# An output projection by seven block products in place of eight

## The chip, the cores and the metric

The kernel runs on one core of one Trainium2 chip. The metric is the device time of one execution in microseconds. A core has five engines with their own instruction queues: PE (matrix products, with its weight loads shown as PEld), DVE (elementwise work), ACT (elementwise functions and copies), POOL (here it issues accumulating DMAs) and SP (it issues DMAs). They meet through semaphores.

## The reference

One layer of a decoder trunk over 512 tokens of width 1024. Five branches mix the tokens; each is projected up to width 1024, gated and summed into `merged`, and one output projection with a residual and a final RMSNorm ends the layer:

```python
gates = jax.nn.sigmoid(gate_logits).reshape(b, s, N_BRANCH, D_MODEL)
merged = jnp.zeros_like(x)
for n, y in enumerate((y_a, y_b, y_c, y_d, y_m)):
    merged = merged + gates[:, :, n] * (y @ w_up[n])
return x + merged @ w_out
...
return rmsnorm(x, final_norm_g)
```

`merged @ w_out` is a product of 512x1024 by 1024x1024. All arrays are float32.

## The kernel before

**Precision.** Each float32 operand f is kept as a pair: hi, f rounded by a copy on ACT, and lo = f - hi, by a subtraction on DVE. A product is three passes on PE, hi by hi, hi by lo and lo by hi (`mm3`, lines 199 to 201). So every block that PE is to read costs one ACT and one DVE instruction first, the split (`split_sb`, lines 217 and 218, for blocks in SBUF).

**Order of the work.** The branches are cut into steps, and the string STEPS lists them. G3 is the next 128 channels of the gate of branch 3 (24 matmuls), U3 the next 128 channels of its up-projection (12 matmuls, then on DVE the product with the gate, line 974, and the addition into `merged`, line 976). dn1 is the last step of branch 3's own scan. After dn1 come one U2, five G3 and eight U3; the last U3 completes channel block 7 of `merged`. Within this order a planner fixes each engine's queue before the run: it goes by the place of an instruction in the text, moved ahead by an offset for some (`PREP` for the splits of weights, `EVAC` for readings of PSUM), and by its own estimate of times. On the chip each queue runs strictly in that order.

**Weights.** A weight block is 128 partitions by 1024, 512 KB. SP loads it into the staging tile `wst`, of which there are two (WST), in the order of the steps; ACT and DVE split its halves into `whi` and `wlo`, of which there are six each (three blocks). For gates (`load_w_add`, lines 171 to 186) ACT copies hi and minus f, and a DMA of POOL's queue with an addition (line 183) makes lo. A slot of `wst` is free when its last copy is done, and a pair of `whi`, `wlo` when PE has used it.

**Output projection** (lines 1036 to 1115). `merged` holds channels on the partitions: 8 blocks of 128 channels by 512 tokens. All eight are split into mH, mL (lines 1062, 217, 218). W_out comes in two column halves of four loads each (`load_out`, line 1043; splits in lines 1050 and 1051 into woH, woL, eleven tiles each). For a column half and each of the four tiles of 128 tokens, eight channel blocks times three passes are summed in one PSUM bank of 128x512; the last token tile of the second half is done in two parts of 256 columns. Then DVE adds the bank to x (line 1085; x lies in the space of `merged`), ACT sums the squares (line 1088), DVE multiplies by the final gain (line 1103), and after the second half the root, its reciprocal and the scaling follow (lines 1092 to 1115), with half of a row scaled on DVE and half on ACT, and two output DMAs.

Of the kernel before, what the change touches and what calls it, by code (L numbers as in the profile page):

```python
# [16 lines left out]
P = 128  # L17
# [47 lines left out]
NWO = 11  # L65
# [16 lines left out]
def build(ctx, tc, x, mem, memT, cols_d, rows_d, wcm, wbv, wcv0, wcv1, wmk, wmv, wup, wout, dw, fg, out):  # L82
# [46 lines left out]
    hpool = ctx.enter_context(tc.tile_pool(name="hpool", bufs=1, side="right"))  # L129
# [17 lines left out]
    def f32(t):  # L147
        return t.bitcast(F32)
# [46 lines left out]
    def mm3(ps, terms, first=True, last=True, check=False):  # L195

        n = len(terms)
        for i, (ah, al, bh, bl) in enumerate(terms):
            mm(ps, lhsT=ah, rhs=bh, start=first and i == 0, stop=False, skip_group_check=check)  # L199
            mm(ps, lhsT=ah, rhs=bl, start=False, stop=False, skip_group_check=check)  # L200
            mm(ps, lhsT=al, rhs=bh, start=False, stop=last and i == n - 1, skip_group_check=check)  # L201
# [13 lines left out]
    def split_sb(f, hi, lo):  # L215

        act(hi, f, AF.Copy)
        V.tensor_tensor(out=lo, in0=f, in1=f32(hi), op=ALU.subtract)
# [730 lines left out]
    upw = {}  # L949

# [12 lines left out]
    def up(n, ys):  # L963
# [6 lines left out]
        mm3(ps, [(*piece(upw[n], 4 * (d % 2) + k, P, 4), *ys[k]) for k in range(NE)])  # L970
# [11 lines left out]
    def step(s):  # L982
# [41 lines left out]
        elif c == "U":  # L1024
            assert None not in ys[i]
            up(i, ys[i])
        else:
# [7 lines left out]

    epool = ctx.enter_context(tc.tile_pool(name="epool", bufs=1))
    mH = epool.tile([P, NK, S], F32R, name="mH")
    mL = epool.tile([P, NK, S], F32R, name="mL")
    nc.sync.dma_start(out=rows[:, :D], in_=fg.broadcast_to([P, D]))

    def load_out(half, k2):
        st = wpool.tile([P, 1056], F32, tag="wst", name="wst", bufs=WST)
        nc.sync.dma_start(out=st[:, :D], in_=wout[half, k2])
        res = []
        for kk in range(2):
            hi = epool.tile([P, S], F32R, tag="woH", name="woH", bufs=NWO)
            lo = epool.tile([P, S], F32R, tag="woL", name="woL", bufs=NWO)
            f = st[:, kk * S:(kk + 1) * S]
            with tc.high_priority(offset=PREP):
                act(hi, f, AF.Copy)  # L1050
                V.tensor_tensor(out=lo, in0=f, in1=f32(hi), op=ALU.subtract)
            res.append((hi, lo))
        return res

    last = ENDS.split()
    wo = []
    for d in range(NK):
        while min(ups.values()) <= d:
            step(last.pop(0))
        if d % 2 == 0:  # L1060
            wo += load_out(0, d // 2)
        split_sb(merged[:, d, :], mH[:, d, :], mL[:, d, :])
    xr, sums, quarter = [], {}, {}

    def parts_of(t):

        return 2 if t == NT - 1 else 1

    for t in range(NT):
        xr.append(merged[:, 2 * t:2 * t + 2, :].rearrange("p a b -> p (a b)"))  # L1070
        nc.sync.dma_start(out=xr[t], in_=x[t * P:(t + 1) * P, :])
    for half in range(2):
        if half:
            wo = [hl for k2 in range(4) for hl in load_out(1, k2)]
        for t in range(NT):
            tsl = slice(t * P, (t + 1) * P)
            parts = parts_of(t) if half else 1
            w = S // parts
            for c in range(parts):
                cs = slice(half * S + c * w, half * S + (c + 1) * w)  # L1080
                ps = pj.tile([P, S], F32, tag="pj", name="pj")
                mm3(ps[:, :w], [(mH[:, k, tsl], mL[:, k, tsl], wo[k][0][:, c * w:(c + 1) * w], wo[k][1][:, c * w:(c + 1) * w])
                                for k in range(NK)])
                xo = xr[t][:, cs]
                V.tensor_tensor(out=xo, in0=xo, in1=ps[:, :w], op=ALU.add)
                ss = epool.tile([P, 1], F32, name=f"ss{t}_{half}_{c}")
                junk = at.tile([P, S], F32, tag="at", name="junk")
                act(junk[:, :w], xo, AF.Square, scale=D ** -0.5, accum_out=ss)
                last = half == 1 and c == parts - 1
                if last:  # L1090
                    root = epool.tile([P, 1], F32, name=f"root{t}")
                    act(root, ss, AF.Sqrt, scale=0.25, bias=quarter[t])

                v = epool.tile([P, 1], F32, name=f"v{t}_{half}_{c}")
                if last:
                    V.tensor_scalar(v, ss, sums[t], 0.25, op0=ALU.add, op1=ALU.mult)
                else:
                    V.tensor_scalar_add(v, ss, sums[t] if half or c else EPS)
                sums[t] = v
                if not last and half == (parts_of(t) > 1):  # L1100
                    quarter[t] = epool.tile([P, 1], F32, name=f"quarter{t}")
                    V.tensor_scalar_mul(quarter[t], v, 0.25)
                V.tensor_tensor(out=xo, in0=xo, in1=rows[:, cs], op=ALU.mult)
            if half == 0:
                continue
# [69 lines left out]
```

## Time and profile before

| | us |
|---|---|
| median of 3 runs | 838.94 (838.84 to 839.29) |
| the profiled execution | 838.62 |
| its span, first to last instruction | 836.6 |
| PE busy | 825.4 |
| DVE busy | 572.6 |
| ACT busy | 490.9 |
| output projection on PE, first to last matmul start | 786.23 to 829.94 |

The profile shows one execution. The span is what its instructions cover; the rest of its time lies around it. Busy times are per engine, and the engines work side by side, so only what an engine makes others wait for counts. In the timeline rows below, the columns are the start, the duration, the engine, the line, the operation, what is written and read, and the count; the idle time of the engine just before and what ended it stand in brackets. The rows of the windows give the stretch, its length, the busy time of PE, PEld, DVE, ACT and POOL with counts, the granted clock of PE, the busy share of the DMA engines and GB/s.

### The profile page before, as it was taken

What the parts mean: (1) busy time and instruction counts of PE and PEld (TensorE: products, weight loads), DVE (VectorE), ACT (ScalarE), POOL (GpSimd) and SP (SyncE); (2) the same over time, 40 slices, a digit from 0 to 9 for tenths busy, and PEclk for the clock granted to TensorE, in tenths of its full rate; (3) what the DMA queues carried; (4) which work ended last, traced back from release to release, by engine and by line L of the source; (5) the groups of instructions that cost most, each with busy time, mean ns of one, the idle gap of its engine ahead of it and who ended that gap; (6) DMA issues with size and microseconds to landing.
All of it is one profiled execution on the core that took longest, in us unless ns stands there. A gap on an engine that the chain in (4) does not pass through costs nothing.

```text
span 836.6 us, 11398 instructions
## 1 busy us (share of the span) xinstructions
PE 825.4 (99%) x4064; PEld 698.0 (83%) x4064; DVE 572.6 (68%) x1098; ACT 490.9 (59%) x892; POOL 104.7 (13%) x155
## 2 busy tenths in 40 slices
PE   8999999999999999999999999999999999999996
PEld 7788888888898889788888888888888888888886
DVE  4879989997456677785676778559657564535644
ACT  6644475635545554667556546586465977884424
POOL 0000020101100232022333000010000201120000
PEclk9999999999999999999999999999999999999999
DMA  9432274345624324336624243474352645685602
GB/s 358 153 128 99 88 153 112 103 125 129 154 95 124 92 89 101 109 96 139 149 90 119 84 139 101 128 170 105 98 142 76 140 121 141 141 180 162 213 34 101
DMA packets 36240, 106.33 MB, mean 127 GB/s; under 512 B 4052, under 2 KB 4180, under 8 KB 36184
## 3 DMA queue, kind: packets, MB, share of 16 engines
q1 hardware_dynamic: 23800, 83.06, 30.0%
q0 software_dynamic: 11520, 20.98, 15.3%
q10 hardware_dynamic: 864, 1.57, 0.5%
q8 instruction: 32, 0.52, 0.3%
q14 instruction: 24, 0.20, 0.1%
HBM read 103.49 MB, written 2.11 MB: 126 GB/s over the span
## 4 chain that ended last, share of the span: by engine, by line
PE 94%; ACT 2%; DVE 1%; DMA 1%; issue 1%; SPq 0%; ACTq 0%
PE pj L201 26%; PE pj L199 26%; PE pj L200 26%; PE pj L530 2%; PE pj L528 2%; PE pj L529 2%; PE po L642 1%; PE wb L628 1%; PE og L833 1%; PE mk L286 1%; PE zb L599 1%; PE zb L598 1%; DMA mt<-in 1%; PE tp L502 0%; DVE hL L322 0%
## 5 line engine op out<-in xcount | busy, mean ns | idle before, releaser
L201 PE MATMUL pj<-hH,wlo 128*128 128x512 f32 x768 | 299.9, 391 | 0.2 <-DVE wlo L163 0.2
L200 PE MATMUL pj<-hL,whi 128*128 128x512 f32 x768 | 299.8, 390 | 0.0
L199 PE MATMUL pj<-hH,whi 128*128 128x512 f32 x768 | 299.6, 390 | 0.1
L162 ACT ACTIVATE whi<-wst 128x512 fp32r<-128x512 f32 (+1 forms) x172 | 107.1, 631 | 163.1 <-PE pj L200 118.3
L201 PEld LDWEIGHTS pj<-hH,wlo 128*128 128x128 f32 x768 | 144.2, 188 | 30.4 <-DVE wlo L163 0.7
L199 PEld LDWEIGHTS pj<-hH,whi 128*128 128x128 f32 x768 | 144.2, 188 | 29.7 <-ACT g L960 0.5
L200 PEld LDWEIGHTS pj<-hL,whi 128*128 128x128 f32 x768 | 144.3, 188 | 29.4
L163 DVE TENSOR_TENSOR wlo<-wst,whi 128x512 fp32r<-128x512 f32 (+1 forms) x172 | 117.1, 687 | 74.4 <-ACT whi L162 74.2
L183 POOL DMA_DIRECT2D wlo<-in x80 | 69.5, 869 | 559.8 <-ACT wlo L182 424.6
L416 DVE SCALAR_TENSOR_TENSOR acc<-u,cols,acc 128x512 f32<-128x512 f32 x120 | 88.7, 747 | 1.4
L184 ACT ACTIVATE whi<-wst 128x512 fp32r<-128x512 f32 x80 | 50.3, 629 | 57.1 <-PE pj L200 41.2
L200 PE MATMUL pj<-yL,whi 128*128 128x512 f32 x160 | 62.5, 390 | 0.0
L199 PE MATMUL pj<-yH,whi 128*128 128x512 f32 x160 | 62.4, 391 | 0.0
L201 PE MATMUL pj<-yH,wlo 128*128 128x512 f32 x160 | 62.3, 390 | 0.0
L182 ACT ACTIVATE wlo<-wst 128x512 fp32r<-128x512 f32 x80 | 49.4, 618 | 5.9 <-PE at L529 4.0
L201 PEld LDWEIGHTS pj<-yH,wlo 128*128 128x128 f32 x160 | 30.1, 188 | 6.2
L199 PEld LDWEIGHTS pj<-yH,whi 128*128 128x128 f32 x160 | 30.0, 188 | 6.1
L200 PEld LDWEIGHTS pj<-yL,whi 128*128 128x128 f32 x160 | 30.1, 188 | 5.9
L618 DVE TENSOR_TENSOR_SCAN kp<-kp 128x512 f32<-128x512 f32 (+3 forms) x32 | 26.9, 859 | 10.8 <-POOL kp L611 10.6
L529 PE MATMUL pj<-wlo,hH 128*128 128x256 f32 (+1 forms) x112 | 31.8, 284 | 0.0
L530 PE MATMUL pj<-whi,hL 128*128 128x256 f32 (+1 forms) x112 | 31.8, 284 | 0.0
L528 PE MATMUL pj<-whi,hH 128*128 128x256 f32 (+1 forms) x112 | 31.5, 283 | 0.0
(310 smaller groups left out, 1232.4 us busy)
## 6 DMA issues: line engine op xcount, KB each, us to landing
wst<-in SPq DMA_DIRECT2D x136, 512.0 KB, 3.4
wlo<-in POOLq DMA_DIRECT2D x80, 256.0 KB, 5.3
xt<-in SPq DMA_DIRECT2D x4, 512.0 KB, 9.0
merged<-in SPq DMA_DIRECT2D x4, 512.0 KB, 3.2
wst<-in SPq DMA_DIRECT2D x2, 528.0 KB, 4.3
mr<-in SPq DMA_DIRECT2D x2, 512.0 KB, 10.7
f<-crow SPq DMA_DIRECT2D x4, 256.0 KB, 6.6
out<-merged SPq DMA_DIRECT2D x4, 256.0 KB, 2.0
```

Source lines behind the costliest of these rows:

```text
L162: act(hi[:, :m], f, AF.Copy)
L163: V.tensor_tensor(out=lo[:, :m], in0=f, in1=f32(hi[:, :m]), op=ALU.subtract)
L182: act(lo[:, :m], st[:, sl], AF.Copy, scale=-1.0)
L183: G.dma_start(out=lo[:, :m], in_=src[:, sl], accum_op=ALU.add)
L184: act(hi[:, :m], st[:, sl], AF.Copy)
L199: mm(ps, lhsT=ah, rhs=bh, start=first and i == 0, stop=False, skip_group_check=check)
L200: mm(ps, lhsT=ah, rhs=bl, start=False, stop=False, skip_group_check=check)
L201: mm(ps, lhsT=al, rhs=bh, start=False, stop=last and i == n - 1, skip_group_check=check)
L416: V.scalar_tensor_tensor(out=a, in0=u[:, k:k + S], scalar=col("a_w", i * 31 + k), in1=a, op0=ALU.mult, op1=ALU.add)
L528: mm(dst[t], lhsT=hH[:, k, tsl], rhs=wh, start=first, stop=False, skip_group_check=True)
L529: mm(dst[t], lhsT=hH[:, k, tsl], rhs=wl, start=False, stop=False, skip_group_check=True)
L530: mm(dst[t], lhsT=hL[:, k, tsl], rhs=wh, start=False, stop=k == NK - 1, skip_group_check=True)
```

## The change

The output projection becomes one level of Strassen's algorithm in Winograd's form. `merged` is cut into token halves by channel halves, a 2x2 matrix of blocks 256x512; W_out into 2x2 blocks of 512x512. Seven block products on sums of blocks replace eight. The operands are a11 (`aH`), a12 and a22 (`bH`: the second four channel blocks, both token halves), s2 and s4 (sums of blocks of `merged`, both token halves in one tile); and of W_out b11 (w0), b21 (w1), n4 (w2 and w3, made of four blocks each), T1, T2, T3 (differences, T1 and T2 formed on the way in w2 and w3) and b22. Each operand of W_out is 128x1024 twice, split as before. A product is 2 token tiles x 4 channel blocks x 3 passes; X, Z, W and Y are pairs of PSUM banks. Two of the products go on summing in X after X was read, and the last one in Y. What is read from a bank is added to x (`take`), and a part of a row that is complete is squared and multiplied by the gain (`finish`).

Sums and splits of `merged` run on DVE and ACT: b and s2 with the offset PREP, s4 behind the last s2. The loads of w0 to w3 become steps between the last gates and up-projections. The second x tiles are loaded by POOL's queue, the first into tiles of the branches' y. s2 and s4 take the space of hH, hL, which the gates no longer need.

```diff
-NWO = 11
+NWO = 6
...
-U2 U2 dn0 G2 G3 G2 U2 U2 dt2 G2 U2 dt3 G3 G2 U2 G3 dn1 U2 G3 G3 G3 G3 U3 U3 U3 U3
-U3 G3 U3 U3 U3
+U2 U2 dn0 G2 G3 G2 U2 U2 dt2 G2 U2 dt3 G3 G2 U2 G3 dn1
...
+U2 G3 w0 G3 w1 G3 w2 G3 U3 w3 U3 U3 U3 G3 U3 U3 U3 U3
...
+    def operand(f):
+        hi = epool.tile([P, D], F32R, tag="woH", name="woH", bufs=NWO)
+        lo = epool.tile([P, D], F32R, tag="woL", name="woL", bufs=NWO)
+        split_sb(f, hi, lo)
+        return hi, lo
...
+    def weights(i):
+        if i < 2:
+            return [operand(block(0, i, u)) for u in range(2)]
+        u = i - 2
+        t1.append(block(1, 0, u, "t1"))
+        minus(t1[u], t1[u], block(0, 0, u))
+        t2.append(block(1, 1, u, "t2"))
+        minus(t2[u], t2[u], t1[u])
+        f = block(0, 1, u)
+        n4.append(operand(minus(f, f, t2[u])))
...
+    for j in range(4):
+        split_sb(merged[:, j, lo_t], aH[:, j, :], aL[:, j, :])
+    for j in range(4):
+        m, n = merged[:, j, :], merged[:, 4 + j, :]
+        with tc.high_priority(offset=PREP):
+            split_sb(n, bH[:, j, :], bL[:, j, :])
+            V.tensor_tensor(out=n[:, hi_t], in0=m[:, hi_t], in1=n[:, hi_t], op=ALU.add)
+            minus(m[:, hi_t], m[:, lo_t], m[:, hi_t])
+            minus(m[:, lo_t], n[:, hi_t], m[:, lo_t])
+            s2_end = split_sb(m, s2H[:, j, :], s2L[:, j, :])
...
+    with behind(s2_end):
+        for j in range(4):
+            m, n = merged[:, j, :], merged[:, 4 + j, :]
+            minus(n[:, lo_t], n[:, lo_t], m[:, lo_t])
+            s4_end = split_sb(n, s4H[:, j, :], s4L[:, j, :])
+    for t in (2, 3):
+        xr.append([merged[:, 2 * t - 4 + n, :] for n in range(2)])
+        for n in range(2):
+            nc.gpsimd.dma_start(out=xr[t][n], in_=x[t * P:(t + 1) * P, n * S:(n + 1) * S])
...
+    with tc.issue_after(up_end[0].ins):
+        product(X, (aH, aL), lo_t, b11, True)
+    T2 = [operand(f) for f in t2]
+    for t in range(2):
+        take(t, 0, X[t])
+    T3 = []
+    with behind(s2_end):
+        for u in range(2):
+            f = block(0, 0, u)
+            T3.append(operand(minus(f, t2[u], f)))
+    product(Z, (bH, bL), lo_t, b21, True)
+    for t in range(2):
+        take(t, 0, Z[t])
+        finish(t, 0)
+    with behind(s4_end):
+        T1 = [operand(f) for f in t1]
+    product(W, (bH, bL), hi_t, n4, True)
+    for t in range(2):
+        take(2 + t, 0, W[t])
+    product(X, (s2H, s2L), lo_t, T2, False)
+    for t in range(2):
+        take(t, 1, X[t])
+    with behind(s4_end):
+        b22 = [operand(block(1, 1, u)) for u in range(2)]
+    product(X, (s2H, s2L), hi_t, T3, False)
+    for t in range(2):
+        take(2 + t, 0, X[t])
+        finish(2 + t, 0)
+        take(2 + t, 1, X[t])
+    Y = banks()
+    product(Y, (s4H, s4L), hi_t, T1, True)
+    for t in range(2):
+        take(2 + t, 1, Y[t])
+        finish(2 + t, 1)
...
+    product(Y, (s4H, s4L), lo_t, b22, False, halves=(1, 2), done=c12)
```

`block(half, k, u)` loads 128x1024 of W_out into `wst` (or into a tile of its own, for t1 and t2); `minus` is one DVE subtraction; `behind(ends)` and `issue_after` put what stands inside behind the named instruction in its engine's queue; `product` runs the matmuls of one block product with `mm3`; `c12` takes and finishes each part of the last product.

More of the change, by code (lines that the diff above doesn't have):

```diff
@@ L200, in mm3 @@
             mm(ps, lhsT=ah, rhs=bl, start=False, stop=False, skip_group_check=check)
-            mm(ps, lhsT=al, rhs=bh, start=False, stop=last and i == n - 1, skip_group_check=check)
+            end = mm(ps, lhsT=al, rhs=bh, start=False, stop=last and i == n - 1, skip_group_check=check)
+        return end
     def proj(c, scale=None):
@@ L1036, in build @@
     epool = ctx.enter_context(tc.tile_pool(name="epool", bufs=1))
-    mH = epool.tile([P, NK, S], F32R, name="mH")
-    mL = epool.tile([P, NK, S], F32R, name="mL")
+    H2 = S // 2
+    aH, aL = (epool.tile([P, 4, H2], F32R, name=n) for n in ("aH", "aL"))
+    bH, bL = (epool.tile([P, 4, S], F32R, name=n) for n in ("bH", "bL"))
     nc.sync.dma_start(out=rows[:, :D], in_=fg.broadcast_to([P, D]))
[L1041 to L1062, printed above, removed]
-    xr, sums, quarter = [], {}, {}
[L1065 to L1105, printed above, removed]
-            rs = epool.tile([P, 1], F32, name=f"rs{t}")
-            V.reciprocal(rs, root)
-            V.scalar_tensor_tensor(out=rs, in0=rs, scalar=sums[t], in1=root, op0=ALU.mult, op1=ALU.add)
-            V.reciprocal(rs, rs)
-            lo_, hi_ = xr[t][:, :512], xr[t][:, 512:]
-            V.tensor_scalar_mul(lo_, lo_, rs)
-            nc.sync.dma_start(out=out[t * P:(t + 1) * P, :512], in_=lo_)
-            act(hi_, hi_, AF.Copy, scale=rs)
-            nc.scalar.dma_start(out=out[t * P:(t + 1) * P, 512:], in_=hi_)
@@ new lines, in block @@
+    def block(half, k, u, tag="wst"):
+        if tag == "wst":
+            t = wpool.tile([P, 1056], F32, tag="wst", name="wst", bufs=WST)[:, :D]
+        else:
+            t = epool.tile([P, D], F32, tag=tag, name=tag, bufs=2)
+        nc.sync.dma_start(out=t, in_=wout[half, 2 * k + u])
+        return t
+    def operand(f):
[3 more added lines that the diff above has]
+        return hi, lo
@@ new lines, in behind @@
+    @contextmanager
+    def behind(ends):
+        with ExitStack() as es:
+            for e in ends:
+                es.enter_context(tc.issue_after(e.ins))
+            yield
+    with behind(s2_end):
[5 more added lines that the diff above has]
+        xr.append([merged[:, 2 * t - 4 + n, :] for n in range(2)])
+        for n in range(2):
+            nc.gpsimd.dma_start(out=xr[t][n], in_=x[t * P:(t + 1) * P, n * S:(n + 1) * S])
@@ new lines, in banks, with product @@
+    def banks():
+        return [pool.tile([P, S], F32, tag=tag, name=tag) for pool, tag in ((pj, "pj"), (at, "at"))]
+    def product(ps, a, sl, b, begin, halves=(1, 1), done=None):
+        for t in range(2):
+            tsl = slice(sl.start + t * P, sl.start + (t + 1) * P)
+            w = S // halves[t]
+            for c in range(halves[t]):
+                cs = slice(c * w, (c + 1) * w)
+                for j in range(4):
+                    wh, wl = (v[:, (j % 2) * S + c * w:(j % 2) * S + (c + 1) * w] for v in b[j // 2])
+                    ah, al = (v[:, j, tsl] for v in a)
+                    mm3(ps[t][:, cs], [(ah, al, wh, wl)], first=begin and j == 0, last=j == 3, check=True)
+                if done:
+                    done(t, cs)
```

72 lines of the change are left out of this document (67 added, 5 removed).

## The prediction

> **What bounds the kernel now.** I read the page's busy times first, then its chain of waits.
>
> ```profile
> PE 825.4 (99%) x4064; PEld 698.0 (83%) x4064; DVE 572.6 (68%) x1098; ACT 490.9 (59%) x892; POOL 104.7 (13%) x155
> PE 94%; ACT 2%; DVE 1%; DMA 1%; issue 1%; SPq 0%; ACTq 0%
> ```
>
> TensorE is busy for 825.4 of 836.6 us, and the chain that ended last is 94% PE. So matmuls that go away shorten the run, unless the stream stops elsewhere. Since a busy PE need not be PE at its peak, I took its rate in the changed stage from the timeline: the first matmul of the output projection, the first of its half-width ones, and the last of all; the groups by line give the counts.
>
> ```profile
> 786.23 0.39 PE L199 MATMUL pj<-woH,mH 128*128 128x512 f32 x1
> 824.31 0.28 PE L199 MATMUL pj<-woH,mH 128*128 128x256 f32 x1
> 829.94 0.28 PE L201 MATMUL pj<-woH,mL 128*128 128x256 f32 x1
> L199 PE MATMUL pj<-woH,mH 128*128 128x512 f32 x56 | 21.8, 389 | 0.0
> L199 PE MATMUL pj<-woH,mH 128*128 128x256 f32 x16 | 4.5, 283 | 0.0
> ```
>
> Each of the lines 199 to 201 has that count, so 168 wide and 48 half-width matmuls. Wide ones start every (824.31 - 786.23)/168 = 0.2267 us, half-width ones every (829.94 - 824.31)/47 = 0.120 us. The stage runs without a gap and takes 168 x 0.2267 + 48 x 0.120 = 43.8 us.
>
> **The part taken away.** Seven products of 2 token tiles x 4 k-blocks x 3 passes make 168 matmuls; the last token tile of the last product is cut in two, so 156 are wide and 24 half-width: 156 x 0.2267 + 24 x 0.120 = 38.2 us. The gain on PE is 43.8 - 38.2 = **5.6 us**, and no more can come from it.
>
> **What the sums add.** In units of 128x512, DVE now does 8 splits of merged, 16 of weights, 8 additions from PSUM and 8 multiplications by the gain: 40. After the change: 14 for splits of merged and its sums, 8 for the sums themselves, 28 for the lower parts of seven 512x512 operands, 16 for the eight differences of weights, 16 additions from PSUM, 8 gains: 90. ACT copies 42 units in place of 24. One unit costs 0.60 us in a row (two take 1.29):
>
> ```profile
> 776.58 1.29 DVE L1051 TENSOR_TENSOR woL<-wst,woH 128x512 fp32r<-128x512 f32 x2
> 770.00:780.00 10.00, 10.00 (x46) 8.29 (x45) 8.60 (x14) 6.23 (x11) 0.00 (x0) 1.00 0.71 230
> 780.00:790.00 10.00, 10.00 (x46) 8.29 (x45) 6.89 (x12) 4.10 (x7) 0.00 (x0) 1.00 0.64 208
> 825.00:830.00 5.00, 5.00 (x44) 5.00 (x42) 2.87 (x11) 2.15 (x6) 0.00 (x0) 1.00 0.17 65
> ```
>
> That is 50 x 0.60 = 30 us more on DVE. No row shows a 128x1024 subtraction; it lies between one unit (0.69) and two (1.29), and I take two. In the windows DVE has 1.4 us free in 770 to 780, 3.1 in 780 to 790, and over half of each later stretch. PE hides the 30 us as long as no product waits for its operand; the first two places to look are the second product and the end.
>
> The second product needs the split of merged's last block, which the last up-projection makes. Before:
>
> ```profile
> 789.22 0.68 DVE L974 TENSOR_TENSOR g<-g,pj 128x512 f32<-128x512 f32 x1
> 791.80 0.69 DVE L218 TENSOR_TENSOR mL<-merged,mH 128x512 fp32r<-128x512 f32 x1 [0.70 <-ACT mH L217]
> ```
>
> It is ready at 792.49, 6.3 us after 786.23. The first product covers 24 x 0.2267 = 5.4 us, and the block comes last of four, 9 matmuls later: it is needed at 793.7. Margin 1.2 us; I cost it at nothing. If DVE is two units later than now, nothing is lost; each further unit shows as a gap.
>
> At the end, two whole tiles and the first half of the last become ready in the last 5.6 us of matmuls, where before it was one tile and a half. The second tile from the start of the second column half shows the price:
>
> ```profile
> 819.41 0.68 DVE L1085 TENSOR_TENSOR merged<-merged,pj 128x512 f32<-128x512 f32 x1
> 822.30 0.49 DVE L1112 TENSOR_SCALAR merged<-merged,rs 128x512 f32<-128x512 f32 x1
> 830.25 0.42 DVE L1085 TENSOR_TENSOR merged<-merged,pj 128x256 f32<-128x256 f32 x1 [1.27 <-PE pj L201]
> ```
>
> DVE is occupied for about 2.5 of those 3.4 us, so 2 x 2.5 + 1.1 = 6.1 us meet 5.6 us of cover: **0.5 us** later than now (bounds 0 and, if the waits of 0.8 us inside each tile are not filled, 2). From 830.25 on the tail is the same work.
>
> **What the earlier weight loads cost.** W_out takes 16 loads of 512 KB in place of 8, and twelve of them are moved up among the last gates: w0 and w1 (two each), w2 and w3 (four each, of which two use the staging buffer wst; the others have tiles of their own). wst has two slots, shared with every gate and up-projection, and SP issues the loads in the order of the program text (in the trace, the issues of lines 153 and 174 follow the list of steps one for one). That is the one resource on the path of PE that the change uses more. Rows of SP, ACT, POOL and PE for the last gates (here G3a, G3b and so on, the five after dn1):
>
> ```profile
> 715.56 0.33 SPq L174 DMA_DIRECT2D wst<-in  x1
> 720.79 0.33 SPq L174 DMA_DIRECT2D wst<-in  x1
> 730.25 0.61 ACT L182 ACTIVATE wlo<-wst 128x512 fp32r<-128x512 f32 x1
> 730.89 0.33 SPq L174 DMA_DIRECT2D wst<-in  x1
> 739.48 0.33 SPq L174 DMA_DIRECT2D wst<-in  x1
> 742.55 0.50 PE L199 MATMUL pj<-hH,whi 128*128 128x512 f32 x1
> 746.95 0.86 POOL L183 DMA_DIRECT2D wlo<-in  x1 [0.17 <-issue]
> wst<-in SPq DMA_DIRECT2D x136, 512.0 KB, 3.4
> wlo<-in POOLq DMA_DIRECT2D x80, 256.0 KB, 5.3
> DMA to landing us min/median/max: 3.7/5.5/9.1
> ```
>
> G3a is loaded at 715.56, and its slot comes free only at 730.86 (then 730.89 is issued): it stood parked until the whi buffers were free. G3b (720.79), G3c (730.89) and G3d (739.48) follow; PE starts G3b at 742.55, so G3c at 748.0 and G3d at 753.4, 24 x 0.2267 each. After the change w0's two loads stand ahead of G3b, w1's ahead of G3c, w2's ahead of G3d: nine loads where there were three. What a slot is held for, unparked, is shown by the W_out loads of before:
>
> ```profile
> 765.68 0.33 SPq L1043 DMA_DIRECT2D wst<-in  x1
> 771.04 1.29 DVE L1051 TENSOR_TENSOR woL<-wst,woH 128x512 fp32r<-128x512 f32 x2 [1.16 <-ACT woH L1050]
> 772.36 1.53 SPq L1043 DMA_DIRECT2D wst<-in  x2
> ```
>
> The first is held from 765.68 to 772.33, 6.6 us; the second from 772.36 to 777.87 (the split at 776.58 above), 5.5 us. With one slot free at 720.8 and one at 730.9, and 5.5 us each, the issues are: w0 720.8 and 726.3, G3b 730.9, w1 731.8 and 736.4, G3c 737.3, w2 741.9 and 742.8, G3d 747.4. From issue to usable a gate takes 3.4 (landing) + 0.6 (copy) + 3.7 to 5.3 (accumulating DMA: the least of line 183's landings in this stretch, the last row, and the page's median) = 7.7 to 9.3 us. G3b and G3c come in time (G3c at 746.6 at the latest, for 748.0); G3d comes at 755.1 to 756.7, for 753.4. So PE stops for 1.7 to 3.3 us; I take the middle, **2.5 us**. By 6.6 us a hold, G3d would be issued at 750.7 and cost 5.0 to 6.6; I take the short hold, since ACT is 70% idle where the late ones lie:
>
> ```profile
> 720.00:730.00 10.00, 10.00 (x46) 8.29 (x45) 3.50 (x5) 9.84 (x15) 1.90 (x3) 1.00 0.69 132
> 730.00:740.00 10.00, 10.00 (x46) 8.29 (x45) 3.48 (x6) 9.91 (x15) 1.98 (x3) 1.00 0.51 107
> 750.00:760.00 10.00, 10.00 (x46) 8.26 (x45) 2.37 (x5) 3.00 (x5) 0.00 (x0) 1.00 0.67 195
> ```
>
> Nothing below zero: the stage has no PE gap to win back. The x loads leave the late SP queue for y's tiles and POOL's queue; POOL has issued its last accumulate before, and x is first added after the first product. I cost them at nothing; each would show as a wait of the PSUM addition.
>
> **The sum**, against the profiled execution's own 838.62 us (span 836.6 and 2.0 around it; the median is 838.94, 0.3 more): 838.62 - 5.6 + 0.5 + 2.5 = 836.0; on the median's footing 836.3. I forecast **836.3 us**.
>
> **The rivals.**
> *All is hidden.* The parked slots give enough room, and DVE keeps up: 838.9 - 5.6 = 833.3 to 834.5. For it: parking of G3a took 15 us of slot time that a load with buffers of its own doesn't need. Against it: nine loads through two slots.
> *The weights come late, and the kernel is slower.* One mechanism: ACT is 98 to 99% busy from 720 to 740 with work that precedes w0 in the text, so w0's copies wait. If w0's first slot is given back at 738 in place of 726, G3b is issued at 738, and PE waits for it until 747 or so, 4 to 6 us; G3c and G3d, two w loads behind each, add about 3 us each: 10 to 12 us in all, so 843 to 845. It decides from about 7 us of stall (5.6 + 1.7) on. For it: the two ACT rows, and the DMA engines, which are 90% busy where the accumulates of three gates meet the loads:
>
> ```profile
> 740.00:750.00 10.00, 9.92 (x44) 7.87 (x44) 5.29 (x8) 8.94 (x15) 4.09 (x5) 1.00 0.90 198
> ```
>
> Against it: the copies of G3b and G3c, which stood in that stretch, move out of it and leave holes. In the last window below the granted clock falls, some 4 us after the last matmul at 829.94; a stop of G3b of that length would bring a spell of slow matmuls too.
>
> ```profile
> 832.00:834.00 2.00, 0.00 (x0) 0.00 (x0) 0.78 (x3) 0.72 (x1) 0.00 (x0) 1.00 0.15 54
> 834.00:836.60 2.60, 0.00 (x0) 0.00 (x0) 0.00 (x0) 0.00 (x0) 0.00 (x0) 0.54 0.42 160
> ```
>
> The Trainium skill, "TensorE: Matmul & The Clock Gate", section "HAM oscillation — how this bites in real kernels", says that a PE gap over about 3.4 us halves the clock, and that it takes as long again to come back; by it, an estimate, this rival would cost 1.7 us more. The trace agrees as far as it goes: 1.00 until 834, 0.54 after.
> *DVE is the bound of the new stage.* With 30 us more and 1.4 to 3.1 us free in each ten around the last up-projections, the split of the last block comes 3 to 5 units late: 1 to 2 us ahead of the second product beyond its margin, and as much at the end: 838 to 840, about no change.
> That the change doesn't do its seven products is excluded by the diff.
>
> **How the numbers follow.** Forecast 0.40 (835 to 837.4), all hidden 0.17, late weights 0.28, DVE the bound 0.15. The range leaves out the far half of the late weights and little else: 833.0 to 843.5. A difference under 0.2% (1.7 us) is about what a measurement can't tell from none. Faster by more (below 837.3): all hidden, most of the forecast: 0.54. Within: DVE's case and edges: 0.19. Slower: 0.27.
>
> **What would show it.** Right: 156 and 24 matmuls at 0.227 and 0.120 us; one PE gap of 2 to 3 us ahead of the last but one gate, released by the accumulating DMA or its ACT copy; no gap between the products; the last DMA about 6.6 us after the last matmul. Wrong: a gap ahead of the first gate after w0 (late weights), no gap at all (all hidden), or PE waiting for DVE's split of b or s4 between the products (DVE).

## The result, and the profile after

The changed kernel takes **864.56 us** (median of 4 runs, 863.77 to 865.54) where the kernel before takes 839.1 beside it: 1.0304 times as long, interval 1.0286 to 1.0322. The forecast was 836.3, with a range to 843.5. The profiled execution took 863.77 us, its span 862.1. Two executions in a slower state, one of e12 (1679.55 us) and one of the kernel before beside e10 to e12 (2150.97 us), are left out of the medians and ratios below. The page's busy times and its chain of waits, after:

```profile
PE 829.0 (96%) x4028; PEld 697.3 (81%) x4028; DVE 601.7 (70%) x1136; ACT 499.6 (58%) x898; POOL 107.2 (12%) x159
PE 79%; issue 11%; DVE 4%; ACT 3%; DMA 2%; POOL 1%; POOLq 0%; SPq 0%; ACTq 0%
```

PE has 36 matmuls fewer, and DVE is busy 29 us more, where 30 were forecast (572.6 to 601.7). But PE's share of the chain falls from 94 to 79%: PE waits now. Where, PE's timeline of the kernel after shows (in brackets the idle time before a matmul, and what ended it). These are its waits from 750 us on, with the first and the last matmul of the output projection between and behind them:

```profile
750.80 0.79 PE L199 MATMUL pj<-hH,whi 128*128 128x512 f32 x1 [8.43 <-ACT whi L184]
754.13 0.79 PE L201 MATMUL pj<-hH,wlo 128*128 128x512 f32 x1 [2.12 <-DMA wlo<-in]
...
766.13 0.50 PE L201 MATMUL pj<-hH,wlo 128*128 128x512 f32 x1 [3.38 <-DMA wlo<-in]
...
777.53 0.79 PE L201 MATMUL pj<-hH,wlo 128*128 128x512 f32 x1 [4.05 <-DMA wlo<-in]
...
797.42 0.50 PE L201 MATMUL pj<-hH,wlo 128*128 128x512 f32 x1 [1.28 <-DMA wlo<-in]
...
812.97 0.39 PE L199 MATMUL pj<-woH,aH 128*128 128x512 f32 x1
...
836.20 0.50 PE L200 MATMUL pj<-woL,s4H 128*128 128x512 f32 x1 [0.68 <-DVE woL L218]
...
853.26 0.39 PE L199 MATMUL at<-woH,s4H 128*128 128x256 f32 x1 [1.86 <-DVE xr1L L1146]
...
854.67 0.28 PE L201 MATMUL at<-woH,s4L 128*128 128x256 f32 x1
```

The span splits in three. The projection begins at 812.97 and not at 786.23: **26.7 us late**. It then takes 41.7 us from first to last matmul where it took 43.7: **2.0 us shorter**, not 5.6. The tail behind the last matmul is 862.1 - 854.67 = 7.4 us, **0.8 longer**. 26.7 - 2.0 + 0.8 = 25.5, the whole of 862.1 - 836.6.

Of the 26.7 us, the five waits are 19.3. Behind three of them matmuls run at half speed for a while; two rows of the same timeline, 0.43 us apart where 0.23 is normal:

```profile
755.15 0.63 PE L200 MATMUL pj<-hL,whi 128*128 128x512 f32 x1
755.58 0.63 PE L201 MATMUL pj<-hH,wlo 128*128 128x512 f32 x1
```

Matmuls start so at 27 places between 754 and 781, 0.2 us too late each, and the steps right behind the waits at 750.80, 754.13 and 777.53 are 0.60 us: 27 x 0.2 + 3 x 0.37 = 6.5 us. That leaves 0.9 for starting up again.

What starves the gates is the queue of SP, whose timeline shows the loads through `wst` after the change (L174 are the gates G3b, G3c and G3d, L1056 the loads of W_out; rows between them left out):

```profile
720.68 10.43 SPq L1056 DMA_DIRECT2D wst<-in  x2
...
744.06 0.33 SPq L174 DMA_DIRECT2D wst<-in  x1
...
745.20 6.42 SPq L1056 DMA_DIRECT2D wst<-in  x2
754.02 0.33 SPq L174 DMA_DIRECT2D wst<-in  x1
760.60 1.51 SPq L1056 DMA_DIRECT2D wst<-in  x2
765.59 0.33 SPq L174 DMA_DIRECT2D wst<-in  x1
```

G3b is issued at 744.06; before it was 720.79, and in the forecast 730.9. w0's two blocks took both slots at 720.7 and 730.8 and gave the first back only at 744. ACT's and DVE's rows say why:

```profile
741.61 2.00 ACT L218 ACTIVATE woH<-wst 128x1024 fp32r<-128x1024 f32 x2 [0.76 <-DVE yL L218]
```

```profile
740.88 0.69 DVE L218 TENSOR_TENSOR yL<-f,yH 128x512 fp32r<-128x512 f32 x1 [0.16 <-ACT yH L218]
742.82 2.35 DVE L218 TENSOR_TENSOR woL<-wst,woH 128x1024 fp32r<-128x1024 f32 x2
```

w0's copy is released by the last DVE instruction of dn1. The tiles `woH` and `woL` are in `epool`, whose space is that of the branches' tiles, and it comes free with that instruction. So the blocks sat in the gates' slots for 23 and 14 us, not 5.5. I first took this parking for the whole cause.

### The profile page after: what moved, and what is told of

Read it like the earlier page. It is cut to its first block, busy times and chain, and to the rows that moved or that the text cites. A ratio compares the mean times of both kernels' runs of the same rounds, so it can differ in the third digit from the quotient of the medians.

```text
span 862.1 us, 11382 instructions
## 1 busy us (share of the span) xinstructions
PE 829.0 (96%) x4028; PEld 697.3 (81%) x4028; DVE 601.7 (70%) x1136; ACT 499.6 (58%) x898; POOL 107.2 (12%) x159
## 4 chain that ended last, share of the span: by engine, by line
PE 79%; issue 11%; DVE 4%; ACT 3%; DMA 2%; POOL 1%; POOLq 0%; SPq 0%; ACTq 0%
PE pj L201 21%; PE pj L200 21%; PE pj L199 21%; DMA wlo<-in 2%; PE pj L530 2%; PE pj L529 2%; PE pj L528 2%; POOL wlo L183 1%; PE po L642 1%; PE wb L628 1%; PE og L833 1%; PE mk L286 1%; PE zb L599 1%; PE zb L598 1%; DMA mt<-in 1%
## 5 line engine op out<-in xcount | busy, mean ns | idle before, releaser
L201 PE MATMUL pj<-hH,wlo 128*128 128x512 f32 x768 | 303.0, 394 | 11.1 <-DMA wlo<-in 10.8
L201 PEld LDWEIGHTS pj<-hH,wlo 128*128 128x128 f32 x768 | 145.7, 190 | 43.6 <-DMA wlo<-in 12.8
L618 DVE TENSOR_TENSOR_SCAN kp<-kp 128x512 f32<-128x512 f32 (+3 forms) x32 | 26.9, 859 | 10.8 <-POOL kp L611 10.6
```

What stands on the lines that cost most here:

```text
L201: end = mm(ps, lhsT=al, rhs=bh, start=False, stop=last and i == n - 1, skip_group_check=check)
```

## The experiments

All are changes of the kernel after, unless said otherwise; ratios are to the kernel before, run beside them. The table reads the first and last matmul of the output projection off each profiled execution (PE's timeline, as above), so that a late start and a long stage are told apart. The starts are of single executions, which differ by up to 3.4 us before the gates in question are reached (the load of G3d in e11 and e12: 739.46 and 742.87), so small differences between them say little.

| | median us | ratio (95%) | stage starts | its length | span |
|---|---|---|---|---|---|
| before | 838.94 | 1 | 786.23 | 43.7 | 836.6 |
| after | 864.56 | 1.030 (1.029 to 1.032) | 812.97 | 41.7 | 862.1 |
| e1 W_out late | 853.55 | 1.018 (1.016 to 1.019) | 789.66 | 55.2 | 851.9 |
| e2 own staging | 846.62 | 1.009 (1.008 to 1.011) | 794.55 | 43.6 | 845.2 |
| e3 before, early loads | 859.17 | 1.024 (1.022 to 1.026) | 807.08 | 43.7 | 857.4 |
| e4 gap filled | 866.47 | 1.032 (1.030 to 1.035) | 815.49 | 42.1 | 864.7 |
| e5 paced | 850.41 | 1.014 (1.013 to 1.016) | 797.43 | 42.5 | 847.1 |
| e6 paced, POOL | 852.86 | 1.017 (1.015 to 1.018) | 798.68 | 44.8 | 851.2 |
| e7 not parked | 861.33 | 1.027 (1.024 to 1.029) | 808.48 | 42.3 | 857.7 |
| e8 no differences | 844.90 | 1.007 (1.005 to 1.008) | 795.26 | 40.8 | 843.6 |
| e9 text order | 846.19 | 1.009 (1.007 to 1.010) | 793.63 | 43.7 | 844.4 |
| e10 x late | 847.37 | 1.009 (1.007 to 1.011) | 797.01 | 41.6 | 845.6 |
| e11 spread | 851.38 | 1.014 (1.011 to 1.017) | 799.24 | 44.0 | 850.4 |
| e12 spread, POOL | 850.94 | 1.016 (1.011 to 1.020) | 802.65 | 45.1 | 854.7 |
| e13 behind U3 | 846.07 | 1.009 (1.008 to 1.011) | 795.59 | 42.0 | 844.6 |
| e14 behind gates | 850.04 | 1.014 (1.013 to 1.016) | 793.01 | 48.1 | 848.2 |
| e15 before, extra loads | 856.51 | 1.022 (1.019 to 1.024) | 804.57 | 43.7 | 855.1 |

### The gates' staging slots: e1, e2, e3

**e1** moves w0 to w3 behind the up-projections:

```diff
-U2 G3 w0 G3 w1 G3 w2 G3 U3 w3 U3 U3 U3 G3 U3 U3 U3 U3
+U2 G3 G3 G3 G3 U3 U3 U3 U3 G3 U3 U3 U3 w0 w1 w2 w3 U3
```

> The seven products as changed, but the four steps w0 to w3 stand after the last gate, ahead of the last U3, so that all gates and up-projections load first. Theory A (w0's two loads hold both wst slots until the space of the branch tiles is free, and the gates behind them starve: 21 us of PE waits and half-clock matmuls after each): no wait of PE on wlo or whi before the last U3; what is left is the 5.6 us gain, about 1 us of tail and a late n4 or b11 of up to 4 us: 833 to 838. Rival B (the bytes or the ACT and DVE work of the W_out operands are too much, wherever they stand): the waits move to the products and the time stays at 850 or more. Rival C (DVE sums of the new stage are the loss): 860, since nothing of that stage changes.

853.55 us. The gates are fed again, and the stage starts 3.4 us late instead of 26.7. But it lasts 55 us, since its operands come late; PE's waits there, from the view of waits (total, times, longest):

```profile
PE pj L199 <- ACT woH L218: 5.4, 4, 4.3
PE pj L200 <- DVE woL L218: 3.7, 2, 1.9
```

So the position of the loads decides, and there is a cost at either end.

**e2** leaves the list as it is and gives W_out two staging tiles of its own:

```diff
-NWO = 6
+NWO = 5
...
-            t = wpool.tile([P, 1056], F32, tag="wst", name="wst", bufs=WST)[:, :D]
+            t = epool.tile([P, D], F32, tag="wos", name="wos", bufs=2)
```

> The order of the changed kernel kept, but W_out blocks are loaded into two staging tiles of their own (in the space of one pair of operand tiles, 5 in place of 6) and not into wst. Theory A: the gates load as before the change, no PE wait at the gates; 833 to 838. Rival B (DMA engines or ACT too full with twelve early loads): PE waits on wlo stay, over 850. Rival C: 860.

846.62 us: **18 of the 25.5 us go** when W_out no longer passes through the gates' slots. The loads are later too, since the new tiles lie in `epool`: the first is issued at 744.63, and after the change at 720.68. No run has staging of its own that is free earlier.

**e3** is the kernel before, without any of Strassen's algorithm, with its first four W_out loads (the steps w0 and w1) among the gates:

```diff
+U2 G3 w0 G3 w1 G3 G3 U3 U3 U3 U3 G3 U3 U3 U3 U3
...
+            for k2 in (2 * i, 2 * i + 1):
+                wo.extend(load_out(0, k2))
```

> The kernel before, without the seven products, but with its four W_out loads of the first half made steps: two right behind the first gate after dn1, two behind the second; the last gate one place earlier, as in the change. Theory A: the first two hold both slots until about 743, PE waits about 10 us at the second gate with half-clock matmuls after it, then 2 to 4 us at the third: 850 to 856. Rivals B and C (the amount of loads, or the sums): 839 to 842.

859.17 us, 20.5 more than before, from the loads alone. Its waits are those of the kernel after:

```profile
PE pj L200 <- DMA wlo<-in: 8.7, 2, 6.6
PE pj L198 <- ACT whi L183: 6.8, 1, 6.8
```

### Is the half clock on the path? e4

34 unused matmuls stand between the gates G3a and G3b, where PE waits 8.4 us:

```diff
+            with tc.issue_after(pend[0].ins):
+                for _ in range(34):
+                    mm(dummy, lhsT=hH[:, 0, :P], rhs=hH[:, 0, :], start=True, stop=True)
```

> The changed kernel with 34 matmuls more, whose result nothing uses, put on PE between the first and the second gate after dn1, so that the longest wait (8.4 us) is filled and the clock should stay full. If the half-clock matmuls after that wait are on the path that sets the end: 21 x 0.2 = 4 us less, 860.4. If the chain of loads through the slots sets when the third gate starts, PE only waits longer there: 863.5 to 865, with the third gate's wait 4 us longer. In both cases the granted clock between 750 and 760 is 1.00 in place of 0.50.

866.47 us, nothing gained, but the run doesn't settle the question. The wait ahead of G3b fell to 1.7 us, and the granted clock from 750 to 760 rose from 0.50 to 0.71, where 1.00 was expected. A gap of 2.5 us stayed, and behind it PE has 13 half-speed steps, as many as after the change; with the later spells there are 31 of them in place of 27. So hardly a slow matmul was taken away, and what a faster clock would give back is not shown. What speaks against a price is the chain of loads. G3c's load is issued at 754.02 (754.92 in e4), right when DVE gives back w1's first block, and G3c's accumulating DMA follows ACT's copy of that load; neither waits for PE, and in both kernels PE then waits 3.38 us for this DMA. By that, which is argued, what slow matmuls don't take there the next wait takes.

### Is it the parking? e7 and e15

**e7** loads w0's and w1's blocks at the same places, but only a small ACT copy reads them, so the slots come back on landing; the operands are split from the gain rows instead.

```diff
+                sg = tpool.tile([P, S], F32, tag="sg", name="sg")
+                act(sg[:, :8], f[:, :8], AF.Copy)
+            return [operand(rows[:, :D]) for u in range(2)]
```

> The changed kernel, in which w0's and w1's loads go to the staging buffer wst at the same places as before, but each is read only by a small ACT copy (8 columns) into a tile outside the space that comes free late; the operands of the two first products are split from the gain rows instead, with the same ACT and DVE work, so the output is not the reference's. Parking theory (the slots are held because the operands' own space is not free until about 743 us): the slots come back on landing, the gates after dn1 are fed, PE's waits for wlo and whi fall from 21 us to under 4, and what is left is the late stage: 843 to 850 us. Rival, ACT's order (w0's copies stand behind other ACT work until about 738 us, whatever their space): the small copies are as late, the waits stay above 10 us, and the time is 853 us or more.

861.33 us: only 3.2 us less in the end, and **my theory of the parking as the whole cause fell**. SP's rows of the gates in e7:

```profile
733.45 0.33 SPq L174 DMA_DIRECT2D wst<-in  x1
...
742.60 0.38 SPq L174 DMA_DIRECT2D wst<-in  x1
...
756.21 0.33 SPq L174 DMA_DIRECT2D wst<-in  x1
```

G3b is 10.6 us and G3c 11.4 us earlier. It helps at first: counted back from the projection's first matmul, the 168th is 4.5 us behind the kernel before, where after the change it is 14.0. Then most of it is lost again. PE waits 14.5 us for `wlo` in all, and the projection starts 22.3 us late. w0's and w1's reads stand in ACT's queue behind the branch's work (one block that was issued at 728.4 was read at 737.4), w2's loads hold the slots from 746.9 and 752.7, and G3d, issued at 739.48 before, comes at 756.21; its copies on ACT then stand behind a copy of W_out that waits 10.5 us for a difference on DVE. In this kernel four operand copies also stand ahead of G3c's copies on ACT, so it is no clean test of parking.

**e15** leaves the new arithmetic out: the kernel before with four extra loads at e3's places, read by the same small copies and not used.

```diff
+                t = wpool.tile([P, 1056], F32, tag="wst", name="wst", bufs=WST)
+                nc.sync.dma_start(out=t[:, :D], in_=wout[0, k2])
+                sg = tpool.tile([P, S], F32, tag="sg", name="sg")
+                act(sg[:, :8], t[:, :8], AF.Copy)
```

> The kernel before, with its own W_out loads in the old place and four extra loads of W_out through wst at the places where e3 has w0 and w1; each extra block is read by one small ACT copy (8 columns, outside the late space) and not used. Against e3: the same loads through the same two slots at the same places, but not parked. Parking theory: the gates are fed about as before, and of e3's 20.5 us at most 5 are left: 839 to 844 us. Rival (the number of loads through two slots and ACT's order): 850 us or more.

856.51 us, only 2.7 better than e3, but the two totals can't be compared, because the edit does more than its expectation says. It also moves the end of the list of steps into the loop that issues W_out's own loads. So these no longer stand in the old place, but among the up-projections: they are issued at 754.75, 764.31, 775.88 and 786.64, and before at 765.68, 772.36, 773.56 and 777.89. e15 has eight loads of W_out there, e3 four.

At the gates it does what parking theory asks: G3b is issued at 734.22, and the waits there are 0.35, 1.92 and 2.32 us, 4.6 in place of e3's 15.5. The 120th matmul ahead of the projection's first, behind these waits, shows what is left of e3's loss (kernel before, e3, e15):

```profile
759.03 0.39 PE L199 MATMUL pj<-yH,whi 128*128 128x512 f32 x1
779.88 0.39 PE L198 MATMUL pj<-hH,whi 128*128 128x512 f32 x1
767.99 0.39 PE L198 MATMUL pj<-yH,whi 128*128 128x512 f32 x1
```

PE is 20.9 us late in e3 and 9.0 in e15, 1.6 of them from ahead of the gates. So here four early loads cost the gates 21 us when they are parked and split, and some 7 when they are read at once and not split. The rest of e15's loss is one later wait of 7.6 us, with PE's row first and ACT's behind it:

```profile
784.04 0.80 PE L198 MATMUL pj<-yH,whi 128*128 128x512 f32 x1 [7.59 <-ACT g L959]
```

```profile
782.26 1.15 ACT L1055 ACTIVATE woH<-wst 128x512 fp32r<-128x512 f32 x2 [5.89 <-DMA wst<-in]
783.32 0.67 ACT L959 ACTIVATE g<-pj,cols 128x512 f32<-128x512 f32 x1
```

A copy of W_out waits at the head of ACT's queue for a load that was issued only at 775.88, and behind it waits the gate's reading of PSUM that PE needs. The copy is of one of the kernel's own loads, which e3 has behind it by then. So this wait says nothing of parking, and no run prices e3's loads unparked over the whole kernel.

### What stays with own staging: e8, e9, e10, e13

In e2 the stage starts 8.3 us late. PE's row, and two of ACT's, show the larger wait:

```profile
759.32 0.80 PE L199 MATMUL pj<-yH,whi 128*128 128x512 f32 x1 [4.28 <-ACT g L961]
```

```profile
755.08 1.06 ACT L218 ACTIVATE woH<-wos 128x1024 fp32r<-128x1024 f32 x1 [8.24 <-DMA wos<-in]
...
758.59 1.25 ACT L961 ACTIVATE g<-pj,cols 128x512 f32<-128x512 f32 x2
```

It is the same picture as in e15: a W_out copy, waiting for its load, ahead of the gate. The load is late since all that waited for the space is issued together. The windows of e2 (busy us of PE, PEld, DVE, ACT and POOL, the granted clock, the share of the 16 DMA engines, GB/s):

```profile
750.00:760.00 10.00, 5.72 (x25) 4.40 (x24) 3.63 (x4) 4.30 (x6) 0.00 (x0) 0.93 1.06 342
...
780.00:790.00 10.00, 10.00 (x45) 8.26 (x45) 10.00 (x15) 2.82 (x5) 0.00 (x0) 1.00 0.32 105
790.00:800.00 10.00, 10.00 (x46) 8.27 (x45) 9.87 (x20) 3.95 (x7) 0.00 (x0) 1.00 0.00 0
800.00:810.00 10.00, 10.00 (x46) 8.29 (x45) 10.00 (x19) 5.37 (x9) 0.00 (x0) 1.00 0.16 54
810.00:820.00 10.00, 8.23 (x36) 6.34 (x35) 10.00 (x17) 6.22 (x8) 2.18 (x4) 1.00 0.37 121
```

The DMA engines are full from 750 to 760, where before they were at 0.67, and DVE is full from 780 to 820, where before it was 69% busy at first and half busy or less then. Each of the next runs tries to take one of these away.

**e8** leaves out the eight differences of blocks of W_out, 8 x 1.22 us of DVE:

```diff
-        minus(t1[u], t1[u], block(0, 0, u))
...
-        n4.append(operand(minus(f, f, t2[u])))
+        n4.append(operand(block(0, 1, u)))
```

> The kernel of e2 (own staging for W_out) with the eight differences of blocks of W_out left out (the operands are split from the blocks as they are; the output is not the reference's): 8 x 1.22 = 9.8 us less on DVE, all else the same, two loads of W_out in each of w2 and w3 the same but for the order of their use. Theory that DVE's load in 780 to 820 us costs PE 3 us of waits and the half clock after them, and that the differences standing in DVE's queue add to the wait of the late gate: 840 to 843 us. Rival, that the bunch of loads alone sets the loss of e2: 845 to 847 us, with the wait of the gate for ACT still above 4 us.

844.90 us. The late gate's wait stays (4.45 us), as the rival had it; the stage falls from 43.6 to 40.8 us, the shortest of all. So DVE's work holds the stage up by up to 3 us, and the late start is not its doing. Some 1.7 of these are the half-speed spell behind e2's wait of 1.77 us in the stage (last section); e10 and e13, with the differences but without that spell, take 41.6 and 42.0. Neither expectation had both.

**e9** puts each load one step ahead of its arithmetic in the list.

```diff
+U2 G3 G3 G3 G3 l0 U3 w0 l1 U3 w1 U3 l2 U3 w2 l3 G3 U3 w3 l4 U3 U3 U3
```

> e2's own staging, with each W_out load issued one step of the list ahead of the arithmetic on it (so that no ACT or DVE instruction of W_out waits for a load at the head of its queue), all of them behind the fourth gate's load, and x's loads after the last of them. If in-order queues behind late loads are the loss in e2 and e5: the gates' waits fall under 2 us, DVE remains full in 780 to 820 us, and the time is 838 to 842 us. If the space, DVE's work or the bytes of the stretch are the limit whatever the order: 845 to 850 us.

846.19 us, as e2. It tests little: SP's rows show x's loads and the four of `t` issued together again at 740 to 749, as in e2, whatever their place in the text.

```profile
739.55 0.42 SPq L1077 DMA_DIRECT2D xr0H<-in  x1
...
745.62 3.10 SPq L1058 DMA_DIRECT2D t<-in  x4
```

Only an order that is demanded of the queue holds. **e10** demands it for x's loads, behind the last gate or up-projection load of the text:

```diff
+            with tc.issue_after(sp_last[0].ins):
+                nc.sync.dma_start(out=xr[t][n], in_=x[t * P:(t + 1) * P, n * S:(n + 1) * S])
```

> The kernel of e2 with x's four loads (1 MB) taken out of the bunch at 740 us and issued behind the last gate or up-projection load, so that they are first in the queue again at about 770 us; nothing else. Theory that the transfers of the bunch, sharing 16 busy DMA engines, set the wait of 4.3 us at 754 to 759 us: 1 MB less in the bunch is some 3 us at 340 GB/s, so the wait falls to about 1 us and the half clock behind it goes: 841 to 843.5 us. Rival, that the wait is the order of ACT's queue whatever the transfers do: 846 to 847 us. If x comes late for its first addition, a new wait of DVE at 795 us shows, and the time is longer.

847.37 us, no better than e2. PE's rows and DVE's:

```profile
757.50 0.50 PE L201 MATMUL pj<-yH,whi 128*128 128x512 f32 x1 [1.92 <-ACT g L963]
...
772.74 0.80 PE L201 MATMUL pj<-yH,whi 128*128 128x512 f32 x1 [4.50 <-DVE g L977]
```

```profile
770.86 1.22 DVE L1068 TENSOR_TENSOR t<-t,wos 128x1024 f32<-128x1024 f32 x1 [3.18 <-DMA wos<-in]
772.00 0.68 DVE L977 TENSOR_TENSOR g<-g,pj 128x512 f32<-128x512 f32 x1
```

The wait of 4.3 us fell to 1.9, as it should with 1 MB less in the bunch. A new one of 4.5 us came 15 us later: now a difference of W_out stands in DVE's queue, waiting for its load, ahead of an up-projection's reading.

**e13** takes that order away: the first differences of w2 and of w3 are put behind such a reading.

```diff
+        with tc.issue_after(read[0].ins):
+            minus(t1[u], t1[u], f0)
```

> e10, with the first difference of W_out in w2 and in w3 put behind the reading of an up-projection's PSUM in DVE's queue (w2 and w3 stand one and two steps later in the list), so that it no longer waits for its load ahead of that reading. Theory (in-order queues behind late loads): the wait of PE for DVE g, 4.5 us at 772 us, goes, and with it the half clock behind it, 2 to 3 us: 838 to 841 us. Rival, that the bytes or DVE's total work set the loss and the wait only moves again: 844 to 848 us.

846.07 us. PE's row in that place:

```profile
774.80 0.50 PE L201 MATMUL pj<-yH,whi 128*128 128x512 f32 x1 [2.18 <-ACT g L964]
```

The wait is halved and comes from another engine: behind the difference in DVE's queue now stands the addition into `merged`, and the gate's reading on ACT waits for that. The rival holds: the wait only moved.

### Other orders: e5, e6, e11, e12, e14

**e5** has own staging, the list `U2 G3 G3 G3 G3 w0 U3 U3 w1 U3 U3 G3 w2 U3 U3 w3 U3 U3`, and on SP each W_out load behind the load before it in the text, x's last:

```diff
+        with tc.issue_after(sp_last[0].ins):
+            sp_last[0] = nc.sync.dma_start(out=t, in_=wout[half, 2 * k + u])
```

> The seven products with W_out loaded into two staging tiles of its own (e2), and besides each W_out load and the first x loads issued behind the load that precedes it in the text, x after the last weight, and the order of the steps changed so that w0 follows the fourth gate: no bunch of loads between 744 and 750. Theory: in e2 the 8 us wait of ACT for a W_out block held up the reading of a gate's bank behind it in ACT's queue, and that cost PE 4.3 us and 2.3 us of half clock: 839 to 841. Rival (DVE, fully busy from 780 to 820, is the bound there and takes back what is won): 844 to 847, with the waits of PE on DVE in the products grown.

850.41 us, worse than e2. PE waits 5.4 us at 774 for DVE `g`, which stands behind a difference that waits for its load.

**e6** is e5 with the eight differences on POOL (`minus(..., G)`).

> As e5, and the eight differences of W_out blocks (128x1024) computed on POOL and not on DVE, 10 us of DVE work less. If DVE is the second bound of the new stage (PE waits 1.8 and 1.1 us for it and 2 to 3 us of half clock in e2): 3 to 6 us under e5, 833 to 837. If not: as e5. If POOL is much slower than DVE or holds DVE up, or holds up the last gate's accumulating DMA, which POOL issues: above e5.

852.86 us, no better than e5. DVE isn't relieved: over the whole run it is busy 603.5 us, in e5 600.5, though 9.8 us of work left it. Its instructions take longer beside POOL's, as a row of each shows:

```profile
772.79 2.95 POOL L1066 TENSOR_TENSOR wos<-wos,t 128x1024 f32<-128x1024 f32 x1
773.00 3.29 DVE L979 TENSOR_TENSOR merged<-merged,g 128x512 f32<-128x512 f32 x1
```

This addition takes 0.69 us elsewhere; here it ends 0.55 us behind POOL's instruction. Behind it stands a gate's reading on ACT, for which PE waits 7.16 us at 777. So the expectation's last case came true, POOL holding DVE up.

**e11** is e10 with w2 and w3 later in the list, and their loads on SP each behind the gate or up-projection load ahead of it; **e12** is e11 with multiplications by the gain on POOL, of which the edit moved only one, not five as its expectation says (it moves the pieces ahead of a token tile's last two, and only one tile has a third).

```diff
+U2 G3 G3 G3 G3 w0 U3 U3 w1 U3 G3 w2 U3 U3 w3 U3 U3 U3
```

> e10, and also the loads of w2 and w3 (eight of 512 KB) spread: w0 and w1 stand behind the fourth gate's load, w2 behind the fifth gate's, w3 two steps later, each of w2's and w3's loads behind the gate or up-projection load ahead of it on SP. If the bytes in 743 to 760 us are what costs (theory), that stretch has two W_out loads where e2 has eight, and the wait there goes altogether: 838 to 841 us, with DVE full in 780 to 820 us as what is left. Rival, DVE's queue: the differences of w2 and w3 wait for loads that come later still, with gates' evacuations behind them, as in e5: 845 us or more with a wait of PE for DVE g.

> e11 with the five multiplications by the gain that are not a token tile's last two on POOL in place of DVE: some 5 x 0.6 = 3 us less on DVE in 795 to 830 us, where it is full. If DVE is what is left there: 1 to 3 us less than e11. If POOL's slower multiplication (a 128x1024 took 2.4 to 3.2 us in e6, so 1.2 to 1.6 us here) holds the tiles back: the same or longer.

851.38 and 850.94 us. In e11 the rival came true, and more so than in e5: PE waits 8.1 us for DVE `g` at 775. e12 says nothing on DVE's load, since one instruction of 0.68 us left it; the intervals of the two overlap.

**e14** is e13 with w0's splits behind the third gate's reading on ACT.

```diff
+U2 G3 G3 G3 w0 G3 w1 U3 w2 U3 w3 U3 U3 G3 U3 U3 U3 U3
...
+            with tc.issue_after(read[1].ins):
+                return [operand(f) for f in fs]
```

> e13, with also w0's four ACT and DVE operations put behind the readings of the third gate's PSUM (w0 one step later in the list, w1 after it), so that w0's late loads hold up no gate on ACT. Theory as in e13: the 1.9 us wait for ACT g at 757 us goes too: 835.5 to 839 us, about 0 to 3 us faster than the kernel before. Rival: w1's and w2's blocks come later by what w0's do, and DVE, full from 780 us on, is late in the products: 841 us or more.

850.04 us. PE's waits ahead of the stage add up to 5.4 us, as in e13 (5.5), but are shorter each, and no half-speed spell follows, where e13 has one of eight steps. The stage starts at 793.0, 2.6 us earlier than in e13 (1.0 of it from before 740). But every block comes later by as much as w0's do, DVE is full from 790 to 820, and the operands of the fifth and sixth products are late: the stage takes 48.1 us. No order that I tried beats the kernel before; the best with the whole computation, e2, e9 and e13, are 7.3 to 7.9 us slower.

## Why the prediction was wrong

**PE's gain: the mechanism was right, not the size in time.** 36 matmuls are gone, and the clean stretches run at the forecast 0.227 us. But the stage shortened by 2.0 us, not 5.6. It takes 41.7 us where 38.2 were forecast: the two waits in it cost about 2.9 us with starting up again, and from 829.29 on the steps are 0.233 us (24 of them take 5.60), which is another 0.5; why they are longer is open.

**DVE's margin, costed at nothing, was the first mistake.** The forecast gave the 30 us of DVE a cover of one product and named as the signs PE waiting for the split of b or s4. The waits came elsewhere: for the additions from PSUM (1.86 us for `xr1L` after; 1.8 and 1.1 in e2) and for the splits of weights. With the gates fed (e2) DVE is full for 40 us and the stage is as long as before, 43.6 us; without the eight differences (e8) it is 40.8, and 41.6 and 42.0 with them where no half-speed spell falls into it (e10, e13). The rival "DVE is the bound of the new stage" described it. Even a start at 786.23 with e13's stage of 42.0 and its tail of 7.1 would end at 835.3, only 1.3 us earlier than before.

**The failed step is the slot hold in "What the earlier weight loads cost".** It took 5.5 us for each load, from rows of W_out loads that had free tiles and an idle ACT, and had G3b issued at 730.9 and G3d at 747.4, for a stall of 2.5 us. After the change they were issued at 744.06 and 765.59, and the waits are 19.3 us. Two things lie in it. The first is that w0's operands had no space until dn1's last instruction, which the forecast did not look at; w0's blocks were held 23 and 14 us. With loads that are read at once, the lateness behind the gates falls from 20.9 to 9.0 us in the kernel before (e3, e15), and at the 168th matmul ahead of the projection from 14.0 to 4.5 us in the kernel after (e7). The second is that every load's hold depends on the ACT queue and on what else arrives: in e7, unparked, the first blocks were held 6.4 and 9.2 us and w2's first 9.3, and the projection still started 22.3 us late. How the 26.7 us divide between the two stays open, since e7 is no clean test. The shorter of two holds was chosen because ACT is idle after 740; but before 740 it was 98% busy, and that is where the first two loads had to get out.

**"The weights come late" was the right rival at half its price.** It put G3b at 738 and the stall at 10 to 12 us. Its reason, ACT's other work, is only a part of what happened: with that alone G3b was issued at 733.45 (e7), and after the change w0's copies stand behind dn1's last work, whose space they need. Its chance of 0.28 was too low for a resource that the forecast itself called the one on PE's path that the change uses more.

**The order on SP** was taken to follow the text. In the kernel after it did, for `wst`; with other tiles (e2, e9) the loads came in another order.

**The tail** cost 0.8 us where 0.5 was forecast. **The half clock** came, as the rival's sentence on the Trainium skill, "TensorE: Matmul & The Clock Gate", section "HAM oscillation — how this bites in real kernels", said of long gaps: the 8.43 us gap is followed by half speed until 760. The estimate by it was 1.7 us; the three spells here make 6.5. Whether they were on the path e4 doesn't show.

**What is shown and what is open.** Shown: with W_out's loads out of the gates' slots, and later, 18 us come back (e2), and early loads through these slots make the kernel before slower too without any of the algorithm (e3); read at once, they cost a third of it at the gates (e15). Shown in e2, e10 and e15: a W_out instruction waiting for its load stands in ACT's or DVE's queue ahead of the reading that PE needs, and moving one such order moves the wait. Open: how much of it is parking in the kernel after, and what the half-speed spells cost. Argued only: that the full DMA engines from 750 to 760 and the full DVE from 780 to 820 leave no order that wins; e10's shorter first wait and e8's shorter stage speak for it, but an order that is better than mine was not excluded.

## What to carry to other kernels

Before a load is moved up through a shared staging buffer, ask of each block when its *destination* is free and what its reader's queue holds at that moment; the hold is the time until then, not the transfer and the copy. A saving in matmuls must be weighed against the stage's next engine over the whole stage, not against the cover of one product. When a wait is taken away, look for the next instruction behind the same late arrival: here it came back on another engine in e10 and e13, and in the stage in e14.

## What the runs showed of the hardware

A short stop was enough for the half clock. In e2 PE's timeline has a step of 2.16 us, and 1.3 us behind it matmuls start 0.43 us apart until 823:

```profile
816.71 0.40 PE L199 MATMUL at<-woH,s4H 128*128 128x512 f32 x1
818.87 0.50 PE L199 MATMUL pj<-woH,s2H 128*128 128x512 f32 x1 [1.77 <-DVE xr0L L1146]
...
820.16 0.63 PE L201 MATMUL pj<-woH,s2L 128*128 128x512 f32 x1
820.59 0.63 PE L199 MATMUL pj<-woH,s2H 128*128 128x512 f32 x1
```

A wait of 1.92 us in e10 (at 757.50) had no such spell. The Trainium skill's section named above puts the bound at gaps of about 3.4 us; e2's is well under it.

A 128x1024 subtraction of float32 took 2.4 to 3.5 us on POOL (the eight of e6) and 1.22 on DVE. The Trainium skill, "GPSIMD Engine Reference", section "4.1 Engine selection", says about twice as slow for two inputs; here it was 1.9 to 2.8 times, with DVE at work beside it. DVE paid for it too: beside POOL's subtractions the addition into `merged` took 3.29 us in place of 0.69 (e6, above), while two multiplications that read PSUM (at 776.22 and 787.60) took 0.67 and 0.68, as elsewhere.

Loads of 512 KB took far longer in a bunch. The page of the kernel after has their median from issue to landing in the last column, and below it stands the view of e2's DMA issues from 739 to 762:

```profile
wst<-in SPq DMA_DIRECT2D x140, 512.0 KB, 3.3
```

```profile
wos<-in SPq DMA_DIRECT2D x4, 512.0 KB, 7.2
t<-in SPq DMA_DIRECT2D x4, 512.0 KB, 13.4
```
